# Conditioning loads moved to GpSimd's queue, the value weights split before the query rotation, and two partial sums of squares added on VectorE

## The chip, the cores and the metric

The kernel runs on one core of a Trainium2 chip. The metric is the device time of one execution in microseconds (us). It works from SBUF, with TensorE (PE) writing into eight PSUM banks; VectorE (DVE), ScalarE (ACT), GpSimd (POOL) and SyncE (SP) work beside it. DMAs are issued from the queues of SP, ACT and POOL, each in the order of the program: an instruction that waits holds everything behind it on its queue.

## What is computed

One encoder block over 1024 tokens of width 1024 in fp32. Two branches share an input projection; their gated sum is projected, and a SwiGLU layer follows. All norms are scaled and shifted by a conditioning vector `ada`.

```python
ada = silu(c) @ w_ada + b_ada                    # 6 x 1024 values
sh1, sc1, gt1, sh2, sc2, gt2 = split(ada, 6)
h = rms(x, g_pre_mix) * (1 + sc1) + sh1
q_lat, kv_lat, k_rope_raw, u, gates = split(h @ w_in)
a = mla(q_lat, kv_lat, k_rope_raw, ...)          # w_uq, w_uk, w_uv, rotation, softmax, w_o
b = s5(u, ...)                                   # state-space scan, gelu, w_glu
x = x + gt1 * rms((sig(gate_a) * a + sig(gate_b) * b) @ w_mix_out, g_post_mix)
h = rms(x, g_pre_ffn) * (1 + sc2) + sh2
x = x + gt2 * rms((silu(g) * up) @ w_ffn_out, g_post_ffn)
```

## The kernel before

Activations lie transposed, channels on partitions, in tiles of 128 channels by 1024 tokens; `halves` are the two times 512 tokens. Every product is made exact by splitting: `mm3` (lines 201 to 203) runs three matmuls, high by high, high by low, low by high. `WStream.split` (lines 183 and 184) casts a raw weight tile to its high half on ACT and subtracts it on VectorE for the low half. `get(ahead)` hands out the next tile and splits up to `ahead` tiles past it; there are two raw buffers and three split ones.

The order on each engine is that of the program, written by hand. Work of other kinds is threaded between the matmuls by generators: `s5_next` runs a step of the state-space branch, `norm_step` a step of the query norm and of the key/value norm.

The stages that the change touches:

- **Beginning** (lines 494 to 580). Eight tiles of x and eight of conditioning weights (`pw`) come in on SP's queue. ACT squares x; VectorE adds pairs; `norm_sums` (line 245) sums over channels with eight 128x1 matmuls for each added pair. `p_mm` (line 490) computes the conditioning of the upper four channel tiles on PE. For the lower four, `cond(k)` reduces two rows of w_ada against silu(c) on VectorE (`ada_reduce`, line 455). `norm_rstd` makes 1/rms, the matmuls of line 529 spread it, `h_prep` and `h_low` make the high and low halves of h. `tables` is a generator with small operations for the state-space branch.
- **Projection tiles 18 to 25** (the loop with `ADA0`, `QN0`). After the matmuls of a tile, `done` takes two sigmoids on ACT (line 954) and stores them; `flush()` issues the loads that `later` has put aside, on ACT's queue (line 147); `ada_do()` reduces the tiles that were asked for one projection tile before (`ada_reduce2`, line 462); then the next are asked for with `ada_load` or `ada_load2`, into buffers that the state-space branch no longer needs (er/ei, mr/mi, tz/r); then `norm_step`.
- **Query, key and value weights.** `uq_nope` makes four tiles of queries, `split_store` (line 1016) evicts each half as a high and a low part and stores both. `uq_rope` makes the rotated part: two tiles on PE, then products with cos and sin on VectorE out of PSUM. `uk_half` and `uv_tiles` (lines 1101 to 1103, eviction in line 1107) alternate on PE. The PSUM pool gives four banks to each of its two tags, taken in turn. `y_chain` puts gelu on ACT and a subtraction on POOL in between.
- **Gate** (`glu`, eight tiles of 48 matmuls): each reduces one conditioning tile and asks for the next with `ada_load`, on POOL's queue but for the first. Attention and the feed-forward layer follow; only the buffer count of one load in attention changes there.

The handover of a conditioning tile, as it stands before:

```python
        proj_tile(i, done)          # two sigmoids and their stores at the end
        flush()                     # issues what later() has put aside, on ACT
        if i >= QN0:
            ada_do()                # VectorE reduces those tiles
            ...                     # ada_load2: later(x, a["wada"][i][:, c])
            norm_step()
```

Of the kernel before, what the change touches and what calls it, by code (L numbers as in the profile page):

```python
# [13 lines left out]
ALU = mybir.AluOpType  # L14
# [6 lines left out]
KD = D // P  # L21
# [69 lines left out]
def _body(tc, a, out):  # L91
# [373 lines left out]
    with ExitStack() as p0:  # L465
        xp = pool("xp", stack=p0)
        x2 = pool("x2", bufs=1, stack=p0)
        tp = pool("s5t", stack=p0)
        sp = tp.tile([P, 96], F32, name="sp")
        SY.dma_start(sp, a["s5a"])  # L470
        xT = xp.tile([P, KD, S], F32, name="xT")
        rs = xp.tile([P, S], F32, name="rs")
        gsc = xp.tile([P, KD], F32, name="gsc")


        PK = KD // 2
        sq = [h_tile(F32, "sq") for _ in range(KD)]
        pw = [h_tile(F32, "pw") for _ in range(KD)]
        ptiles = [i for k in range(PK, KD) for i in (8 + k, k)]

        def p_load(*js):
            for j in js:
                SY.dma_start(pw[j], a["wadk"][ptiles[j]])

        def p_mm(*js):
            for j in js:
                i = ptiles[j]
                o = i - 8 - PK if i >= 8 else i
                for k in range(KD):
                    PE.matmul(pada[:, o:o + 1], pw[j][:, k * P:(k + 1) * P], silc[:, k:k + 1],  # L490
                              start=(j == 0 and k == 0), stop=(j == KD - 1 and k == KD - 1))

        for k in range(4):
            SY.dma_start(xT[:, k, :], a["xT"][k])
        p_load(0, 1)
        for k in range(4, KD):
            SY.dma_start(xT[:, k, :], a["xT"][k])
        p_load(2, 3)
        SY.dma_start(sil, a["c"].partition_broadcast(P))
        nxt = [[ada_tile(x2, 8), ada_tile(x2, 0)]]  # L500
        win.load(1)
        p_load(4, 5)
        win.load(1)
        p_load(6, 7)
        SY.dma_start(dd, a["s5d"])

        sums = ps_s5()
        prs = [ps_s5(), ps_s5()]
        pada = ps_s5()
        tables = s5_tables(tp, sp)  # L510
        next(tables)
        A_.activation(silc, vecs[:, 85:93], AF.Silu)
        for k in range(KD):
            A_.activation(sq[k], xT[:, k, :], AF.Square)
            if k % 2:
                tt(sq[k], sq[k - 1], sq[k], ALU.add)
                norm_sums(sums, sq[k], k == 1, k == KD - 1)
            if k == 3:
                next(tables)
                p_mm(0, 1)  # L520
        A_.activation(sil, sil, AF.Silu)
        dg = [x2.tile([P, HF], F32, name="dg", tag="dg", bufs=2) for _ in range(2)]
        rc = norm_rstd(sums, D, NJ)
        for h in range(2):
            norm_diag(rc[:, 4 * h:4 * h + 4], dg[h])
        next(tables)
        p_mm(2, 3)
        for h in range(2):
            PE.matmul(prs[h], ones, dg[h], start=True, stop=True)
            A_.copy(rs[:, halves[h]], prs[h])  # L530
        p_mm(4, 5, 6, 7)
        hhi, hlo = zip(*((h_tile(F32R, "hhi"), h_tile(F32R, "hlo")) for _ in range(KD)))

        def cond(k):
            ada_reduce(x2, nxt[0].pop(0), 8 + k)
            yield
            ada_reduce(x2, nxt.pop(0)[0], k)
            stt(gsc[:, k:k + 1], ada[:, 8 + k:9 + k], 1.0, g_pre[:, k:k + 1], ALU.add, ALU.mult)

        def h_prep(k, cs=(slice(0, S),)):  # L540
            for c in cs:
                stt(xT[:, k, c], xT[:, k, c], gsc[:, k:k + 1], rs[:, c], ALU.mult, ALU.mult)
                A_.activation(hhi[k][:, c], xT[:, k, c], AF.Identity, bias=ada[:, k:k + 1])

        def h_low(k, cs=(slice(0, S),)):
            for c in cs:
                stt(hlo[k][:, c], xT[:, k, c], ada[:, k:k + 1], hhi[k][:, c].bitcast(F32), ALU.add, ALU.subtract)

        for _ in cond(0):
            pass  # L550
        uw = [win.get(0, 0)]
        win.load(1)
        nxt.append([ada_tile(x2, 9), ada_tile(x2, 1)])
        h_prep(0, halves)
        uw.append(win.get(0, 0))
        h_low(0, halves)
        win.load(1)
        nxt.append([ada_tile(x2, 10), ada_tile(x2, 2)])
        win.keep[3] = lambda: [x2.tile([P, D], F32R, name=n) for n in ("w3hi", "w3lo")]
        uw.append(win.get(0, 0))  # L560
        for _ in cond(1):
            pass
        nxt.append([ada_tile(x2, 11), ada_tile(x2, 3)])
        uw.append(win.get(0, 0))
        tt(ada[:, 8 + PK:8 + KD], pada[:, 0:PK], b_ada[:, 8 + PK:8 + KD], ALU.add)
        tt(ada[:, PK:KD], pada[:, PK:KD], b_ada[:, PK:KD], ALU.add)
        stt(gsc[:, PK:KD], ada[:, 8 + PK:8 + KD], 1.0, g_pre[:, PK:KD], ALU.add, ALU.mult)
        h_prep(1)
        ups = [[f() for _ in range(2)] for f in (ps_mm, ps_mm, ps_s5, ps_s5)]
        for k in range(KD):  # L570
            if k:
                cd = cond(k + 1) if k + 1 < PK else iter(())
                next(cd, None)
                h_low(k)
                for _ in cd:
                    pass
                if k + 1 < KD:
                    h_prep(k + 1)
                for _ in range((0, 0, 0, 1, 2, 2, 2, 2)[k]):
                    next(tables, None)  # L580
            if k == 4 or k == 5:
                win.load(1)
            for m in (range(4) if k < KD - 1 else (3, 0, 1, 2)):
                for h, c in enumerate(halves):
                    mm3(ups[m][h], uw[m], hhi[k][:, c], hlo[k][:, c], k, k == 0, k == KD - 1)
        for _ in tables:
            pass
# [354 lines left out]
    def ada_load2(tags):  # L942

        i = ada_rest.pop(0)
        t = [s5b.tile([P, 512], F32, name=n, tag=n, bufs=tags[2]) for n in tags[:2]]
        for x, c in zip(t, halves):
            later(x, a["wada"][i][:, c])
        ada_live.append((t, i))

    for i in range(10, 26):  # L950
        def done(ps, i=i):
            for h in range(2):
                t = ev.tile([P, HF], F32, name="ev", tag="ev")
                A_.activation(t, ps[h], AF.Sigmoid)
                A_.dma_start(gdram[i - 10, :, h * HF:(h + 1) * HF], t)
        proj_tile(i, done)
        flush()
        if ADA0 <= i < QN0:
            ada_do()
            if i < QN0 - 1:  # L960
                ada_load(ADAN, nr, "nr", None, None)
        if i >= QN0:
            ada_do()
            for tags, first in ADA_TAGS:
                if first <= i < 25:
                    ada_load2(tags)
            if i == QN0:
                norms.append(q_norm())
            if i == KN0:
                norms.append(kv_stats())  # L970
            norm_step()
# [18 lines left out]
    yp = pool("y", side="right", stack=y_es)  # L990
    kvp = pool("kv", stack=r_es)
    rp = pool("rp", stack=r_es)
    sg = pool("sg", bufs=3, stack=r_es)
    csb = [rp.tile([P, S], F32, name=f"cs{i}") for i in range(2)]
    G.memset(vhi[:, :, :, 64:66].bitcast(F32), 1.0)
    G.memset(vlo[:, :, :, 64:66].bitcast(F32), 0.0)
# [69 lines left out]

    def uq_rope():

        w = win.get()
        pss = [dense_tile(w, i, 3, qhi, qlo) for i in range(2)]  # L1070
        qr = [qkd["qr"][e].rearrange("(h a r) s -> a h r s", a=2, r=16) for e in range(2)]
        yield
        prev = []
        for h, c in enumerate(halves):
            for i, op in enumerate((ALU.subtract, ALU.add)):
                ti = rp.tile([P, HF], F32, name="qra", tag="qra", bufs=3)
                u = rp.tile([P, HF], F32, name="qrb", tag="qrb")
                tt(ti, pss[i][h], csb[0][:, c], ALU.mult)
                tt(u, pss[1 - i][h], csb[1][:, c], ALU.mult)
                tt(ti, ti, u, op)  # L1080
                prev.append((ti, SCALE, [qr[e][i][:, :, c] for e in range(2)]))
                if len(prev) > 1:
                    split_store(*prev.pop(0))
            yield
        for p in prev:
            split_store(*p)
# [31 lines left out]
    def glu(m):  # L1118
# [2 lines left out]
        pa = dense_tile(w, 0, 4, yhi, ylo)  # L1121
        pg = dense_tile(w, 1, 4, yhi, ylo)
        ada_do()
        ada_load(min(GLU_ADA[m], len(ada_rest) - 8), gp, "wada", 3, G if m else None)
        flush()
        gb = gbs.pop(m)
        sgm = gp.tile([P, S], F32, name="sgm", tag="sgm")
# [191 lines left out]
    for i in range(len(steps) + LAG):  # L1319
# [14 lines left out]
            max_row(mh_)  # L1334
        if i in ATT_ADA:
            ada_do(1)
            ada_load(min(1, len(ada_rest) - 8), gp, "wada", 3)
        if i == NJ:
            gp_es.close()
            op = pool("o", side="right", stack=o_es)  # L1340
# [472 lines left out]
```

## Time and profile before

| | us |
|---|---|
| median of 3 runs | 1736.61 (1736.26 to 1737.35) |
| the profiled execution | 1737.2 |
| its span, first to last instruction | 1735.4 |

The profile is of one execution. Its page gives busy times by engine and by line; the trace behind it can be asked for waits (who waited for whom), timelines (instructions in order of time, with the idle time before each and what ended it), windows (busy time and granted TensorE clock of a stretch) and tiles. All times of the trace count from the span's start. In the rows, PE is TensorE's matmuls, an engine name with a q is its queue of DMA issues, `x32` counts merged instructions, and `L245` is line 245 of the kernel. Durations of neighbouring matmuls overlap; their pace is the distance between starts. The granted clock is 1.00 at 2.4 GHz and 0.50 at 1.2 GHz.

### The profile page before, as it was taken

To read this page: it belongs to the slowest core of one execution; us is meant where nothing else is said; L and a number is where in the kernel's file an instruction comes from. 1 tells how busy PE (TensorE), PEld (TensorE's weight loads), DVE (VectorE), ACT (ScalarE), POOL (GpSimd) and SP (SyncE) were. 2 spreads that over 40 slices of the span, in tenths; PEclk is the share of its full clock that TensorE was granted. 3 is DMA by queue.
4 is the path that set the end of the run, shared out by engine and by line. 5 is a ranking of instruction groups with operands and counts; after the bars stand their busy time and mean duration, and the time that the engine had idled before them with its cause. 6 is when DMAs were issued, how large, how long until landed. Compare 5 with 4: busy or idle time off the path is not lost.

```text
span 1735.4 us, 19440 instructions
## 1 busy us (share of the span) xinstructions
PE 1639.5 (94%) x7486; PEld 1325.3 (76%) x7486; DVE 976.7 (56%) x1613; ACT 553.1 (32%) x743; POOL 147.9 (9%) x191
## 2 busy tenths in 40 slices
PE   7989999986869999999999999999999999999995
PEld 7868887875648867776777777888888888888875
DVE  4978898844574777885455565222322322323367
ACT  3242312222252147767233344321111121111243
POOL 0340000000031000000233220000000000000002
PEclk9899999987889999999999999999999999999998
DMA  6342333452878541420443252212211111111234
GB/s 260 121 119 96 111 102 96 132 171 93 277 233 265 153 126 34 98 44 13 153 133 128 79 200 94 99 58 72 71 55 52 61 38 48 60 32 46 83 119 148
DMA packets 92540, 189.67 MB, mean 109 GB/s; under 512 B 19992, under 2 KB 36504, under 8 KB 92448
## 3 DMA queue, kind: packets, MB, share of 16 engines
q1 hardware_dynamic: 57920, 120.62, 22.8%
q10 hardware_dynamic: 31424, 58.34, 9.7%
q0 software_dynamic: 3104, 9.47, 1.8%
q8 instruction: 59, 0.97, 0.2%
q14 instruction: 33, 0.27, 0.1%
HBM read 148.61 MB, written 39.78 MB: 109 GB/s over the span
## 4 chain that ended last, share of the span: by engine, by line
PE 69%; DVE 17%; DMA 5%; ACT 5%; issue 3%; ACTq 1%; SPq 0%; DVEq 0%; POOLq 0%
PE mm L203 17%; PE mm L202 17%; PE mm L201 17%; DVE t L66 4%; PE sc L1251 2%; PE sc L1252 2%; PE sc L1253 2%; DVE wlo L66 2%; PE pv L1277 1%; PE pv L1276 1%; PE pv L1278 1%; ACT whi L183 1%; PE mm L1390 1%; PE mx L1199 1%; PE s L245 1%
## 5 line engine op out<-in xcount | busy, mean ns | idle before, releaser
L202 PE MATMUL mm<-mh,whi 128*128 128x512 f32 x736 | 288.9, 393 | 4.9 <-DVE mh L74 3.1
L203 PE MATMUL mm<-mh,wlo 128*128 128x512 f32 x736 | 288.9, 393 | 2.2 <-DVE wlo L66 2.1
L201 PE MATMUL mm<-mh,whi 128*128 128x512 f32 x736 | 289.6, 394 | 0.3 <-ACT whi L183 0.3
L66 DVE TENSOR_TENSOR wlo<-wraw,whi 128x1024 fp32r<-128x1024 f32 (+1 forms) x128 | 155.9, 1235 | 77.9 <-ACT whi L183 77.9
L66 DVE TENSOR_TENSOR silu<-mm,silu 128x512 f32<-128x512 f32 x44 | 30.4, 692 | 277.1 <-PE mm L203 270.9
L183 ACT CAST whi<-wraw 128x1024 fp32r<-128x1024 f32 (+1 forms) x128 | 129.9, 1035 | 165.0 <-PE mm L202 137.0
L202 PEld LDWEIGHTS mm<-mh,whi 128*128 128x128 f32 x736 | 139.0, 189 | 38.1 <-DVE mh L74 6.9
L203 PEld LDWEIGHTS mm<-mh,wlo 128*128 128x128 f32 x736 | 139.1, 189 | 33.1 <-DVE wlo L66 4.3
L201 PEld LDWEIGHTS mm<-mh,whi 128*128 128x128 f32 x736 | 139.3, 189 | 30.8 <-ACT whi L183 0.9
L201 PE MATMUL mm<-hhi,whi 128*128 128x512 f32 x384 | 159.1, 414 | 1.2 <-ACT ev L600 1.2
L202 PE MATMUL mm<-hlo,whi 128*128 128x512 f32 x384 | 154.5, 402 | 3.9 <-DVE hlo L74 3.9
L203 PE MATMUL mm<-hhi,wlo 128*128 128x512 f32 x384 | 154.8, 403 | 0.0
L201 PE MATMUL mm<-fhi,whi 128*128 128x512 f32 x304 | 118.8, 391 | 0.0
L202 PE MATMUL mm<-flo,whi 128*128 128x512 f32 x304 | 118.5, 390 | 0.0
L203 PE MATMUL mm<-fhi,wlo 128*128 128x512 f32 x304 | 118.3, 389 | 0.0
L66 DVE TENSOR_TENSOR mr<-mm,mr 128x512 f32<-128x512 f32 (+1 forms) x88 | 56.3, 641 | 97.1 <-PE mm L203 97.0
L66 DVE TENSOR_TENSOR plo<-p,phi 128x1024 fp32r<-128x1024 f32 x64 | 78.3, 1224 | 38.6 <-ACT phi L1257 38.3
L1609 ACT CAST fhi<-silu 128x512 fp32r<-128x512 f32 x44 | 27.3, 620 | 220.6 <-DVE silu L66 220.6
L202 PEld LDWEIGHTS mm<-hlo,whi 128*128 128x128 f32 x384 | 74.4, 194 | 21.8 <-DVE hlo L74 4.8
L201 PEld LDWEIGHTS mm<-hhi,whi 128*128 128x128 f32 x384 | 74.7, 194 | 19.9 <-issue 2.1
L203 PEld LDWEIGHTS mm<-hhi,wlo 128*128 128x128 f32 x384 | 74.1, 193 | 18.1
L1256 ACT ACTIVATE p<-sc 128x1024 f32<-128x1024 f32 x64 | 65.7, 1026 | 63.2 <-PE sc L1253 63.2
(517 smaller groups left out, 2951.2 us busy)
## 6 DMA issues: line engine op xcount, KB each, us to landing
wraw<-in_wfi SPq DMA_DIRECT2D x58, 512.0 KB
wraw<-in_win SPq DMA_DIRECT2D x26, 512.0 KB
wraw<-in_wfo SPq DMA_DIRECT2D x20, 512.0 KB
gdram<-ev ACTq DMA_DIRECT2D x32, 256.0 KB
wada<-in_wada POOLq DMA_DIRECT2D x15, 512.0 KB, 5.3
wraw<-in_wmix SPq DMA_DIRECT2D x10, 512.0 KB
xT<-in_xT SPq DMA_DIRECT2D x8, 512.0 KB
pw<-in_wadk SPq DMA_DIRECT2D x8, 512.0 KB
```

What stands on the lines that cost most here:

```text
L66: return self.eng.tensor_tensor(o, a, b, op=op)
L183: A_.copy(hi, t)
L201: PE.matmul(ps, whi[:, c], rhi, start=first, stop=False)
L202: PE.matmul(ps, whi[:, c], rlo, start=False, stop=False)
L203: PE.matmul(ps, wlo[:, c], rhi, start=False, stop=last)
L245: PE.matmul(ps[:, j:j + 1], src[:, j * P:(j + 1) * P], ones[:, 0:1], start=first and j == 0, stop=last and j == w - 1)
L1199: PE.matmul(pieces[j], qt["qhi"][b][0:96, t * P:(t + 1) * P], qt["khi"][b][0:96, halves[j]], start=True, stop=True)
L1251: PE.matmul(ps[:, c], kh[0:97, kc], qh[0:97, c], start=True, stop=False)
L1252: PE.matmul(ps[:, c], kh[0:96, kc], ql[0:96, c], start=False, stop=False)
L1253: PE.matmul(ps[:, c], kl[0:96, kc], qh[0:96, c], start=False, stop=True)
L1256: A_.activation(p, ps, AF.Exp)
L1609: A_.copy(fh[:, c], t)
```

## The change

1. Beginning: of the four added pairs of squares, the first two are added to the second, and that to the third, on VectorE (`sq[3] += sq[1]`, `sq[5] += sq[3]`), so that `norm_sums` runs for two tiles and not four. A step of `tables` is moved in front of `norm_rstd`. The conditioning tiles 9, 1 and 10 are asked for with the first loads, 2, 11 and 3 one at a time behind the weight tiles. `cond(0)` and the split of the first weight tile move in front of the spreading of 1/rms.
2. Projection tiles 18 to 25: `ada_load` and `ada_load2` issue on GpSimd's queue at once, in place of `later`.
3. `uq_rope` takes its weights with `get(2)`, which splits the tiles of w_uk and w_uv before the rotation. The store buffers of `split_store` go from three to five of each kind, the gate's conditioning buffers from three to one.

```diff
+        nxt += [[ada_tile(x2, 9), ada_tile(x2, 1)], [ada_tile(x2, 10)]]
         SY.dma_start(dd, a["s5d"])
...
             A_.activation(sq[k], xT[:, k, :], AF.Square)
             if k % 2:
                 tt(sq[k], sq[k - 1], sq[k], ALU.add)
-                norm_sums(sums, sq[k], k == 1, k == KD - 1)
+            if k == 3 or k == 5:
+                tt(sq[k], sq[k - 2], sq[k], ALU.add)
+            if k >= 5 and k % 2:
+                norm_sums(sums, sq[k], k == 5, k == KD - 1)
             if k == 3:
                 next(tables)
                 p_mm(0, 1)
         A_.activation(sil, sil, AF.Silu)
+        next(tables)
         dg = [x2.tile([P, HF], F32, name="dg", tag="dg", bufs=2) for _ in range(2)]
         rc = norm_rstd(sums, D, NJ)
         for h in range(2):
             norm_diag(rc[:, 4 * h:4 * h + 4], dg[h])
-        next(tables)
         p_mm(2, 3)
+        for _ in cond(0):
+            pass
+        uw = [win.get(0, 0)]
+        win.load(1)
+        nxt[1].append(ada_tile(x2, 2))
         for h in range(2):
             PE.matmul(prs[h], ones, dg[h], start=True, stop=True)
             A_.copy(rs[:, halves[h]], prs[h])
         p_mm(4, 5, 6, 7)
...
-        for _ in cond(0):
-            pass
-        uw = [win.get(0, 0)]
-        win.load(1)
-        nxt.append([ada_tile(x2, 9), ada_tile(x2, 1)])
         h_prep(0, halves)
         uw.append(win.get(0, 0))
         h_low(0, halves)
         win.load(1)
-        nxt.append([ada_tile(x2, 10), ada_tile(x2, 2)])
+        nxt.append([ada_tile(x2, 11)])
...
-        nxt.append([ada_tile(x2, 11), ada_tile(x2, 3)])
+        nxt[-1].append(ada_tile(x2, 3))
...
         for x, c in zip(t, halves):
-            later(x, a["wada"][i][:, c])
+            G.dma_start(x, a["wada"][i][:, c])
...
-                ada_load(ADAN, nr, "nr", None, None)
+                ada_load(ADAN, nr, "nr", None)
...
-    sg = pool("sg", bufs=3, stack=r_es)
+    sg = pool("sg", bufs=5, stack=r_es)
...
-        w = win.get()
+        w = win.get(2)
         pss = [dense_tile(w, i, 3, qhi, qlo) for i in range(2)]
...
-        ada_load(min(GLU_ADA[m], len(ada_rest) - 8), gp, "wada", 3, G if m else None)
+        ada_load(min(GLU_ADA[m], len(ada_rest) - 8), gp, "wada", 1, G if m else None)
...
-            ada_load(min(1, len(ada_rest) - 8), gp, "wada", 3)
+            ada_load(min(1, len(ada_rest) - 8), gp, "wada", 1)
```

## Rows read from the trace of the kernel before

**Rows 1.** The page, part 1: engine, busy us, share of the span, instructions

```profile
PE 1639.5 (94%) x7486; PEld 1325.3 (76%) x7486; DVE 976.7 (56%) x1613; ACT 553.1 (32%) x743; POOL 147.9 (9%) x191
```

**Rows 2.** Waits of PE, 355 to 530 us: engine, line, waited for: us, times, longest

```profile
PE s L1101 <- ACT whi L183: 12.8, 1, 12.8
PE s L245 <- DVE vi L66: 7.0, 1, 7.0
PE s L871 <- DVE t L66: 6.5, 1, 6.5
PE mm L871 <- DVE gb L66: 4.7, 1, 4.7
PE s L245 <- DVE t L66: 4.2, 1, 4.2
PE mm L203 <- DVE wlo L66: 3.8, 2, 3.3
PE s L1102 <- DVE wlo L66: 2.1, 1, 2.1
PE mm L201 <- issue: 0.5, 1, 0.5
```

**Rows 3.** Timeline of ACT and DVE near 390 us; waits of all engines, 355 to 530

```profile
386.52 0.44 ACTq L147 DMA_DIRECT2D er<-in_wada  x1
...
391.55 0.69 DVE L462 SCALAR_TENSOR_TENSOR er<-er,sil 128x512 f32<-128x512 f32 x1 [17.39 <-DMA er<-in_wada]
...
DVE er L462 <- DMA er<-in_wada: 39.7, 5, 17.4
```

**Rows 4.** Windows: stretch, its length, PE busy (instructions), granted clock, DMA share, GB/s

```profile
374.60:379.90 5.30, 5.30 (x14) 0.50 0.55 175
397.60:400.40 2.80, 2.79 (x5) 0.50 0.10 17
419.90:427.40 7.50, 7.42 (x21) 0.50 0.27 87
445.20:448.10 2.90, 2.88 (x7) 0.50 0.90 278
459.30:465.10 5.80, 5.73 (x10) 0.50 0.85 284
499.10:502.70 3.60, 3.56 (x8) 0.50 0.79 275
540.00:560.00 20.00, 20.00 (x88) 1.00 0.99 254
```

**Rows 5.** Timeline of the beginning, PE, DVE, ACT: start, us, engine, operation, idle before

```profile
10.27 6.98 PE L245 MATMUL s<-ones,sq 128*128 128x1 f32 x32 [10.27 <-DVE sq L66]
41.15 10.55 PE L490 MATMUL s<-silc,pw 128*128 128x1 f32 x64
...
30.94 0.17 DVE L71 TENSOR_SCALAR nq<-s 128x8 f32<-128x8 f32 x1 [10.40 <-PE s L245]
42.95 1.23 DVE L66 TENSOR_TENSOR wlo<-wraw,whi 128x1024 fp32r<-128x1024 f32 x1 [2.79 <-ACT whi L183]
...
14.40 1.06 ACT L514 ACTIVATE sq<-xT 128x1024 f32<-128x1024 f32 x1 [2.78 <-DMA xT<-in_xT]
```

**Rows 6.** Timeline of DVE and ACT around the query rotation, 480 to 501 us

```profile
482.11 0.68 DVE L66 TENSOR_TENSOR qra<-mm,cs 128x512 f32<-128x512 f32 x1
493.17 0.68 DVE L66 TENSOR_TENSOR qrb<-s,cs 128x512 f32<-128x512 f32 x1
500.14 0.68 DVE L74 SCALAR_TENSOR_TENSOR sglo<-mm,sghi 128x512 fp32r<-128x512 f32 x1
...
495.17 1.98 ACT L183 CAST whi<-wraw 128x1024 fp32r<-128x1024 f32 x2
```

**Rows 7.** Tile wada, 500 to 700 us, its landings; timeline of DVE in the gate

```profile
DMA to landing us min/median/max: 5.3/7.5/10.7
...
564.02 0.69 DVE L66 TENSOR_TENSOR sgm<-mm,sgm 128x512 f32<-128x512 f32 x1 [4.51 <-ACT sgm L1129]
```

More of the change, by code (lines that the diff above doesn't have):

```diff
@@ L504, in _body, with cond @@
         p_load(6, 7)
+        nxt += [[ada_tile(x2, 9), ada_tile(x2, 1)], [ada_tile(x2, 10)]]
         SY.dma_start(dd, a["s5d"])
+        def cond(k):
+            ada_reduce(x2, nxt[0].pop(0), 8 + k)
+            yield
+            ada_reduce(x2, nxt.pop(0)[0], k)
+            stt(gsc[:, k:k + 1], ada[:, 8 + k:9 + k], 1.0, g_pre[:, k:k + 1], ALU.add, ALU.mult)
         sums = ps_s5()
@@ L532, in _body @@
         hhi, hlo = zip(*((h_tile(F32R, "hhi"), h_tile(F32R, "hlo")) for _ in range(KD)))
[L534 to L538, printed above, removed]
         def h_prep(k, cs=(slice(0, S),)):
```

## The prediction, made before the changed kernel was run

> **What bounds the kernel now.** I read the page first: TensorE (PE) is busy 94% of the span [rows 1], so the time lies where PE waits or runs slowly. The view of PE's waits, asked stretch by stretch, then shows where that is. In 355 to 530 us PE waits 42 us, in eight groups [rows 2]; before it (110 to 355) the same view lists under 3 us, and after it 3.1 us up to 700. This stretch holds the last projection tiles, the query and key/value (kv) norms, and the weights w_uq, w_uk, w_uv. The windows at the places behind these waits show the second half of the loss: the granted clock is 0.50, the lower of the two levels (1.2 GHz), for 2.8 to 7.5 us after each long wait, while an undisturbed stretch passes 88 matmuls in 20 us, 0.227 each, at 1.00 [rows 4]. At the lower level a 512-column matmul starts every 0.427 us (seen in the timeline as the starts of neighbours), so 47% of such a stretch is lost.
>
> Why PE waits is seen on VectorE (DVE) and ScalarE (ACT), not on PE. A conditioning tile (ada) is loaded by ACT's queue in flush(), which stands behind the two sigmoids of the next projection tile, and ada_do() stands right behind that flush: so VectorE meets the reduction before its load has been in flight at all. ACT issues er at 386.52 and DVE starts its reduction at 391.55 after 17.39 us idle; in all it waits 39.7 us in five places for er alone [rows 3]. VectorE works in order, so the norm's sums, 1/rms, diagonals and the low halves of weights stand behind each wait, and PE waits for exactly these (t, vi, gb, wlo in [rows 2]). The largest single wait, 12.8 us, is for the high half of w_uv: its cast runs at 495.17, last in an ACT queue that first serves gelu and query rotation [rows 2, 6].
>
> **Part 1, the beginning.** PE starts with 128x1 matmuls, 32 instructions in 6.98 us (0.218 each), and is never idle from 10.27 until the projection starts [rows 5]. Two of four sums (8 matmuls, 16 instructions, 3.49 us each) go: 6.98 off PE. Two adds of 128x1024 come to VectorE, 1.23 us each by the nearest operation of that size [rows 5], beside ACT's squares. PE now starts with p_mm(0, 1), whose weights are queued between the fourth and fifth block of x; the blocks arrive 1.3 us apart and the fifth is used at 14.40 [rows 5], so the first of the two is there at about 11.8: 1.5 us later than PE starts now. p_mm(0, 1) ends at 18.8. VectorE reaches its second sum at 20.3 (the add ending at 12.9, the new add, the table chunk of 3.8 us, two adds), so PE idles 1.5 us. 6.98 - 1.5 - 1.5 leaves 3.5 us, carried through p_mm(2, 3) to the spread of 1/rms. The table chunk put ahead of norm_rstd (3.0 us) and its sines go into the 10.40 us in which VectorE waits for that sum anyway [rows 5]; without this cover they would cost their 3.0. cond(0) fits beside p_mm(2, 3). The split of the first weight tile, now done between the copies of rs and the first scaling (VectorE idles 2.79, then 1.23 of work [rows 5]), is moved ahead: the scaling starts right behind the second copy, 2.1 us earlier. The three early ada loads queue behind all of p_load, where the DMA engines are free after some 31 us; they cost nothing there, and take two loads out of the way of the fourth weight tile. From the first scaling to the last low half of h VectorE is the chain, so both gains reach the end of the stage: **5.5 us**. Bounds: p_mm(4..7) now takes 10.55 for 64 instructions [rows 5]; at the 0.218 of the earlier ones it takes 13.9 and eats 3.4. So 2 to 6.
>
> **Part 2, ada loads on GpSimd's queue.** In these tiles POOL has only memsets, so each load goes out as soon as its buffer is free, which is when the reduction of the tile before has read it: one projection tile (48 matmuls, 11 us) ahead of its use. What waits behind them on POOL: the memset of vhi, the cos/sin and kr loads, first needed some 20 us later. The nearest landings of the same tensor from POOL are 5.3, median 7.5, at most 10.7 us [rows 7]; I take 7.5 (same queue, same source, half the size here); even 10.7 is under 11. Followed tile by tile with the durations of the trace: VectorE reduces at 364, as soon as its own queue lets it; the sum of the second half is ready at 368.9 where PE arrives at 368.5; the diagonal of q at 380 against PE at 384; kv's sum at 396.5 against 396.6; the low half of the first w_uq tile at 412.4 against 415.8; kv's diagonal at 424 against 423.6. So PE keeps 0.6 us of wait, and the clock should stay up. What is lost there now: 4.2 + 6.5 + 7.0 + 3.3 + 4.7 = 25.7 us of waits [rows 2], and of half clock 47% of 5.3, 2.8, 7.5, 2.9 and of the first 3.8 of 5.8 us, 10.5, with 0.9 for the sums right before the first of these: 11.4 us [rows 4]. 25.7 + 11.4 - 0.6 = **36.5 us**. The two loads before tile 20 give nothing: VectorE is next held by PE's block kernel at 341. Bounds: at 10.7 us the second lot of four tiles lands at 420, the diagonal is 2 us late and the clock falls once: 33; nothing waits at all: 37.
>
> **Part 3, w_uv split ahead, and five store buffers.** get(2) puts one more cast (1.0 [rows 6]) and subtraction (1.2) ahead of the rotation; w_uv's load is issued behind the split of the third w_uq tile, a good ten us before, and hides. From the end of kv's spread (463.1) to the gate (521.2) PE loses 18.5 us now: 12.8 + 2.1 + 0.5 (3.8 less 3.3) and 0.5 of issue [rows 2] and 2.6 of half clock [rows 4]. The high half no longer waits, so PE runs w_uk and w_uv for five units of 1.36 us; then it needs PSUM tiles that the rotation holds. VectorE frees those of the second half with the multiply that starts 11.1 us after the first (493.17 against 482.11 [rows 6]); the first eviction of w_uk now comes 18 us behind the rotation's start, 1.2 less with one split fewer behind it [rows 6]. So a wait of 5.4 us stays, with some 4 us of half clock behind it (1.9): 7.3 remain, **11 us** gained. Bounds: 4 (PE stands until the first eviction) to 16 (no wait). The buffers (3 to 5 for stores, 3 to 1 for the gate's ada tile) cover waits of ACT and VectorE for stores, during which PE runs on from 463 to 480 out of spare PSUM: nothing counted, and nothing lost if that cover goes but the same waits as now.
>
> **The sum.** 5.5 + 36.5 + 11 = 53.0. The profiled execution took 1737.2 (span 1735.4 and 1.8 around it), 0.6 over the median of the runs: 1737.2 - 53.0 = 1684.2.
>
> **Rivals.** *A, the loads land late.* GpSimd builds them beside a working VectorE and behind one another in order; if two of the five waits return at 5 us each with their clock, 14 us are lost: 1698. For: landings up to 10.7 [rows 7]. Against: 8 us of slack in most tiles. The Trainium skill (SBUF — State Buffer, "SBUF: two separate sides") speaks against this change: while VectorE runs a two-port operation, GpSimd cannot write descriptors, and a load from its queue stands still. By that rule the reductions here, with two SBUF inputs, hold only GpSimd's reads, so the sum would stand, and only copies and scalar operations between them would bring A; the landings of 5.3 to 10.7 beside such work agree with a mild hold at most.
> *B, the rotation holds everything.* w_uk and w_uv are evicted behind it in order; then part 3 gives 0 to 4: 1693.
> *C, another queue is only another queue.* Loads are no earlier in effect, ACT only loses 26 issues of 0.45 us that hide nothing: part 2 is 0, 1737.2 - 16.5 = 1721. Against: the 17.39 us wait begins long before its issue [rows 3]. The Trainium skill (DMA: Bandwidth & Descriptors, "Issuing engines are not separate DMA queues") says that only the time of issue is saved, usually little; that rule is this rival.
> *D, slower: one buffer for the gate's ada tile.* Each of seven loads now starts after the reduction before it and is due 9.5 us later (a gate tile of 48 matmuls at 0.227 less 1.4). VectorE then idles 4.51 us for ACT [rows 7], so landings to 14 us are free. Every us beyond costs 7; it outweighs 53.0 from 21.6 us, twice the largest landing seen; at 22.5, 1744.
>
> **How the numbers follow.** Forecast 0.66 (1678 to 1698, from the bounds of 39 to 59 together); A 0.14; B 0.12; C 0.05; D 0.03. The range 1672 to 1706 takes in the forecast, A and B, and leaves C and D out. A measurement here can tell 0.2% (3.5 us) from no change: faster 0.96, same 0.01 (D just short of its point), slower 0.03.
>
> **What the profile will show.** Right: no VectorE wait for er over 2 us; PE's waits on t, vi, gb under 1 us and the clock at 1.00 from 365 to 440; the gate starting some 53 us earlier; a PE wait of about 5 us between w_uv tiles. Wrong: a PE wait above 3 us before the query rotation (part 2), PE idle until the first eviction of w_uk (part 3), the projection's first matmul after 50 us (part 1), or VectorE waiting for wada in the gate (D).

## The result, and the profile of the changed kernel

| | before | changed |
|---|---|---|
| median of the runs compared, us | 1736.98 | 1684.56 (1677.54 to 1687.83) |
| ratio, 95% interval | | 0.9691, 0.966 to 0.9723 |
| the profiled execution, us | 1737.2 | 1684.47 |
| its span, us | 1735.4 | 1682.7 |

The change is 52.4 us faster; the forecast was 1684.2 out of a sum of 53.0. Where the time went is read from the page first, then from PE's waits of the same stretch as [rows 2].

The first part of the page (engine, busy us, share of the span, instructions); [rows 1] answer to it:

```profile
PE 1618.4 (96%) x7454; PEld 1309.0 (78%) x7454; DVE 977.7 (58%) x1615; ACT 552.5 (33%) x743; POOL 164.0 (10%) x221
```

PE's waits from 355 to 530 us, and windows (stretch, length, busy us and instructions of PE, PEld, DVE, ACT, POOL, granted clock, DMA share, GB/s):

```profile
PE s L1105 <- DVE qra L66: 5.2, 1, 5.2
PE mm L201 <- DVE sglo L74: 0.2, 1, 0.2
PE s L245 <- DVE t L66: 0.2, 1, 0.2
```

```profile
360.00:380.00 20.00, 19.82 (x94) 15.91 (x94) 8.76 (x26) 5.14 (x9) 2.15 (x4) 0.91 0.68 226
380.00:400.00 20.00, 20.00 (x96) 16.45 (x95) 17.34 (x39) 9.05 (x15) 6.72 (x13) 1.00 0.59 192
400.00:431.00 31.00, 31.00 (x134) 24.73 (x133) 23.24 (x60) 10.39 (x17) 3.94 (x9) 1.00 0.98 305
440.00:446.00 6.00, 1.58 (x7) 0.96 (x6) 5.96 (x6) 1.42 (x3) 2.88 (x2) 0.86 0.87 313
446.00:450.00 4.00, 3.25 (x8) 2.58 (x9) 3.84 (x6) 3.97 (x6) 1.74 (x1) 0.50 0.52 194
450.00:455.00 5.00, 4.98 (x20) 3.69 (x19) 4.48 (x6) 1.55 (x5) 0.88 (x1) 0.89 0.67 221
470.00:490.00 20.00, 20.00 (x88) 16.08 (x87) 10.69 (x14) 6.06 (x8) 5.75 (x5) 1.00 0.80 229
```

Of the eight groups of [rows 2], 42 us, one of 5.2 us is left that counts: the wait of the w_uv tiles for the query rotation, which the forecast had kept at 5.4. The granted clock is 1.00 where [rows 4] show 0.50, with two exceptions. One is the fall around that wait (0.86, 0.50 and 0.89 from 440 to 455). The other is short: in the window with 0.91 the clock is 0.60 and 0.55 from 362 to 366, right behind the 128x1 matmuls of the query norm's sum. A second execution of the same kernel (after_again below) has 1.00 from 360 to 380.

Why the others are gone is seen on POOL and VectorE (timeline: start, us, engine, line, operation, idle before it and what ended it):

```profile
356.33 0.54 POOL L951 DMA_DIRECT2D er<-in_wada  x1 [9.37 <-DVE er L462]
361.76 0.68 DVE L462 SCALAR_TENSOR_TENSOR er<-er,sil 128x512 f32<-128x512 f32 x1
381.04 0.68 DVE L462 SCALAR_TENSOR_TENSOR er<-er,sil 128x512 f32<-128x512 f32 x1
```

A load leaves POOL as soon as VectorE has read the buffer, and VectorE starts the reductions of er without a bracket, that is, without idle time: its 39.7 us of waits for er in [rows 3] are zero.

The start of stages in the traces of all kernels is used below, so it is shown once how it is read: the tile view of `yhi`, the gate's input, gives the first and last start of the gate's matmuls, first before, then changed.

```profile
L201 PE MATMUL mm<-yhi,whi x64: 392/398/401, 521.2 to 612.8; 128*128 128x512 f32 x64
```

```profile
L201 PE MATMUL mm<-yhi,whi x64: 392/398/401, 464.8 to 556.4; 128*128 128x512 f32 x64
```

With the tiles of h, kv and the attention scores in the same view, the span falls into five stretches (us, one profiled execution each):

| kernel | to the first projection matmul | to the first w_uk matmul | to the gate | to the first scores | to the end |
|---|---|---|---|---|---|
| before | 51.6 | 429.4 | 40.2 | 98.8 | 1115.4 |
| changed | 47.8 | 386.8 | 30.2 | 98.8 | 1119.1 |
| p1_only | 50.7 | 429.6 | 41.0 | 98.8 | 1117.1 |
| p2_only | 53.9 | 388.8 | 40.6 | 98.8 | 1124.9 |
| get2_only | 51.1 | 432.8 | 31.3 | 98.8 | 1117.4 |
| bufs_back | 48.2 | 388.7 | 31.3 | 98.8 | 1125.1 |
| after_again (changed) | 50.6 | 385.1 | 29.9 | 98.8 | 1123.3 |
| act_at_once | 50.8 | 397.8 | 29.8 | 98.8 | 1116.6 |
| pool_at_flush | 47.3 | 386.5 | 30.1 | 98.9 | 1122.3 |
| rot_late | 47.3 | 391.1 | 28.6 | 111.2 | 1123.9 |
| ylo_dve | 51.2 | 390.4 | 28.0 | 98.8 | 1126.2 |
| row_on_sp | 50.3 | 389.1 | 30.3 | 98.8 | 1113.1 |
| more_pool_loads | 54.2 | 430.8 | 40.2 | 98.8 | 1115.5 |
| before_row_on_sp | 54.2 | 429.5 | 40.8 | 98.8 | 1112.4 |

Before against changed, stretch by stretch: 3.8 + 42.6 + 10.0 + 0.0 - 3.7 = 52.7 us, the difference of the spans. Stretches with the same code differ by some 3 us between executions, so a column is read with that much doubt. In the first column the reason is seen: the last 64 of the 128x1 matmuls before the projection take 10.5 to 10.8 us in six of the executions and 13.65 in the other eight, with the old beginning (51.1 and 51.6 against 53.9 to 54.2) as with the new (47.3 to 48.2 against 50.3 to 51.2). Why there are two durations stays open. The last column is not flat either: the changed kernel gives 3.7 us of its gain back behind the first scores, where the change edits only a buffer count. That is followed up below.

### The profile page after: what moved, and what is told of

Same layout as the page of the kernel before. It is cut to its first block, busy times and chain, and to the rows that moved or that the text cites. A ratio compares the mean times of both kernels' runs of the same rounds, so it can differ in the third digit from the quotient of the medians.

```text
span 1682.7 us, 19415 instructions
## 1 busy us (share of the span) xinstructions
PE 1618.4 (96%) x7454; PEld 1309.0 (78%) x7454; DVE 977.7 (58%) x1615; ACT 552.5 (33%) x743; POOL 164.0 (10%) x221
## 3 DMA queue, kind: packets, MB, share of 16 engines
q0 software_dynamic: 5632, 17.86, 3.5%
## 4 chain that ended last, share of the span: by engine, by line
PE 65%; DVE 20%; ACT 5%; DMA 4%; issue 4%; ACTq 1%; SPq 0%; DVEq 0%; POOLq 0%
PE mm L203 17%; PE mm L202 17%; PE mm L201 17%; DVE t L66 5%; DVE wlo L66 2%; PE sc L1255 1%; PE sc L1256 1%; PE sc L1257 1%; PE pv L1281 1%; PE pv L1280 1%; PE pv L1282 1%; ACT whi L183 1%; DMA mxd<-mneg 1%; PE mx L1203 1%; DVE s L695 1%
```

## The experiments

Each ratio is to the kernel before, timed beside it on the same chip.

### The parts alone

p1_only is item 1 of the change on the kernel before, p2_only its item 2, get2_only this line of item 3:

```diff
-        w = win.get()
+        w = win.get(2)
         pss = [dense_tile(w, i, 3, qhi, qlo) for i in range(2)]
```

> The kernel before with the changed beginning alone (part 1). The forecast's 5.5 us gives 1737.0 - 5.5 = 1731.5. The trace of the changed kernel has the steps behind this stage 6.6 us earlier, which gives 1730.4 if all of it comes from part 1. Rival: the waits behind the beginning swallow it and nothing is left, 1737.0. The view of DVE in the beginning should show the first scaling of h some 7 us earlier.

> The kernel before with part 2 alone, the conditioning loads of the projection tiles issued on GpSimd's queue. The forecast's 36.5 us gives 1700.5. Rival C (another queue is only another queue): 1737.0. Rival A (two of five waits come back): 1714.5. No wait of DVE for er over 2 us, PE at a granted clock of 1.00 from 365 to 440 but for short dips.

> The kernel before with the split of w_uk and w_uv ahead of the query rotation alone (the one edit of get(2), buffers as before). The forecast's 11 us gives 1726.0, with a wait of PE of 5.4 us left between the tiles of w_uv. Rival B (PE stands until the first eviction of w_uk): a gain of 0 to 4 us, 1733.0 to 1737.0.

| | median, us | ratio, 95% interval | gain out of 1742.89 | forecast |
|---|---|---|---|---|
| p1_only | 1738.21 | 0.997, 0.9956 to 0.9984 | 5.2 (2.8 to 7.7) | 5.5 |
| p2_only | 1707.32 | 0.9797, 0.9779 to 0.9816 | 35.4 (32.1 to 38.5) | 36.5 |
| get2_only | 1734.5 | 0.9955, 0.9936 to 0.9973 | 7.8 (4.7 to 11.2) | 11 |

All three forecasts lie within the intervals, the third at its edge; rivals B (0 to 4 us for part 3) and C (0 for part 2) fall, and A for part 2 (1714.5) too. The trace of get2_only shows its mechanism plainly; PE's waits from 355 to 530, where 12.8 for `whi` stood in [rows 2]:

```profile
PE s L1101 <- DVE qra L66: 5.4, 1, 5.4
PE mm L871 <- DVE gb L66: 4.6, 1, 4.6
```

w_uv no longer waits for its cast but for the rotation, 5.4 us as forecast, and the wait for gb, which belongs to part 2, stands untouched. p1_only's own trace does not show its gain at the gate: the gate starts at 521.3 (before: 521.2), and PE's waits from 355 to 530 add up to 46 us in place of 42. So in that execution the waits behind the beginning swallowed the lead, as the rival said. Its time was 1739.0; the kernel before took 1737.2 in the profiled execution and 1737.3 to 1747.4 beside p1_only, so one pair of traces cannot decide 5 us. That part 1 gains is shown by the times alone.

The three gains sum to 48.4 us. The changed kernel was timed again on the chip of the next experiments: 1689.42 against 1743.48, 0.9695 (0.967 to 0.972), 53.2 us. The sum is 4.8 us short of that, which the intervals allow to be chance; but what is missing from the three kernels is the buffers, so these were tried.

> The changed kernel once more, beside the next three on one chip. The first comparison gave 0.9691 of the kernel before (0.966 to 0.9723). Three parts alone gave 5.2, 35.3 and 7.8 us, 48.3 together, and the changed kernel with the old buffers 0.9717: if the buffers matter, this run lies 4.5 us under the one with the old buffers (0.9691 against 0.9717 of the kernel before); if not, both are equal and the sum of the parts misses 5 us that only the parts together give.

### The buffers

```diff
-    sg = pool("sg", bufs=5, stack=r_es)
+    sg = pool("sg", bufs=3, stack=r_es)
-        ada_load(min(GLU_ADA[m], len(ada_rest) - 8), gp, "wada", 1, G if m else None)
+        ada_load(min(GLU_ADA[m], len(ada_rest) - 8), gp, "wada", 3, G if m else None)
```

(and the same in attention)

> The changed kernel with the buffers as before (three store buffers of each kind, three gate tiles). The forecast counts the buffers at nothing: 1684.6, the time of the changed kernel. Rival: the store buffers hold the rotation and part 3 needs them: 2 to 5 us slower, 1686.6 to 1689.6. Rival D would show here as faster: the gate's single buffer costs some of the seven loads, 1 to 10 us.

1693.36 us, 0.9717 (0.9696 to 0.9739). Against the changed kernel's 0.9695 the times alone can't decide, since the intervals overlap. The traces can: the first matmul of w_uq starts at 408.4 without the added buffers and at 408.3 in the changed kernel, and the gate at 468.2 and 464.8, so 3.3 us are lost in between (in after_again that stretch takes 56.2 us, in the changed kernel 56.5, without the buffers 59.8). All engines' waits from 400 to 440 us, first with the old buffers, then in the changed kernel from 400 to 436:

```profile
DVE sglo L74 <- DMA qnd<-sglo: 9.8, 2, 8.6
ACT sghi L1020 <- DMA qnd<-sghi: 9.4, 3, 7.5
...
PE mm L201 <- issue: 2.1, 1, 2.1
```

```profile
ACT kvhi L887 <- DMA qnd<-sghi: 2.5, 1, 2.5
DVE sglo L74 <- DMA qnd<-sglo: 2.4, 1, 2.4
```

With three store buffers ACT and VectorE stand 7.5 and 8.6 us before they can evict the query tiles, and PE loses 2.1 us in front of the next ones; with five, 2.5 and 2.4 us of such waits are left and PE loses nothing. The buffers are worth about 3 us, the expectation's rival (2 to 5); the forecast's nothing was wrong.

### Queue or moment of issue

Part 2 changes two things: the queue, and that the load is issued where it is asked for and not put aside until the next flush. act_at_once keeps ACT's queue and the early place; pool_at_flush takes POOL's queue and the late place.

```diff
-            G.dma_start(x, a["wada"][i][:, c])
+            A_.dma_start(x, a["wada"][i][:, c])
```

```diff
-            G.dma_start(x, a["wada"][i][:, c])
+            later(x, a["wada"][i][:, c], G)
```

(and likewise for the two tiles in `nr`; in pool_at_flush also for the gate's first load)

> The changed kernel with the conditioning loads of the projection tiles back on ACT's queue, but issued at once where they are asked for, not put aside until the next flush. Theory of the forecast (the moment of issue counts, not the queue): er still lands before it is due, the wait of DVE for er stays under 2 us each, and the time is the changed kernel's, 1684.6, or a few us over it where ACT stands for the buffer that VectorE has yet to read. Rival (only GpSimd's own queue does it, because ACT's is blocked either way): er waits and half clock return, up to 1684.6 + 36 = 1720.

> The changed kernel with these loads put aside until the flush as before, but issued there on GpSimd's queue. GpSimd has nothing in between that waits for the sigmoids, so its instructions run ahead of that place in the program: the loads should go out at the same moment as in the changed kernel, and the time is the same 1684.6. Rival: the place in the program decides, the loads go out a tile later and some 36 us return, 1720.

act_at_once: 1693.0, 0.9721 (0.9697 to 0.9745). pool_at_flush: 1692.26, 0.9709 (0.9682 to 0.9736). In the trace of pool_at_flush the loads leave at the same moments as in the changed kernel (the row shown above stood at 356.33), though the program asks for them a projection tile later:

```profile
346.60 0.54 POOL L148 DMA_DIRECT2D er<-in_wada  x1 [24.87 <-DVE t L66]
357.05 0.54 POOL L148 DMA_DIRECT2D er<-in_wada  x1 [9.38 <-DVE er L463]
```

So the place in the program is nothing by itself: an engine with nothing else to do runs ahead to it. On ACT the early place does most of the work: VectorE's waits from 340 to 470 us list none for er. But ACT, which has work of its own, now stands where the load must wait for its buffer. ACT's waits from 355 to 440 and PE's from 355 to 530:

```profile
ACT whi L183 <- DMA ei<-in_wada: 4.6, 1, 4.6
ACT qhi L887 <- DMA ei<-in_wada: 4.3, 1, 4.3
```

```profile
PE s L245 <- DVE vi L66: 3.0, 1, 3.0
PE s L245 <- DVE t L66: 2.3, 1, 2.3
```

Casts stand behind the issue, VectorE behind the casts, PE behind VectorE, and the granted clock falls to 0.83 on the average of 365 to 385. The first w_uk matmul comes at 448.6 against 435.7 in after_again, 12.9 us later. In p1_only, which has the same beginning and the old loads, it comes at 480.3, 44.6 us later than in after_again. Of these the moment of issue brings 31.7 (some 2 of them are the buffers': that matmul comes at 436.9 in bufs_back and at 434.6 in the changed kernel), and an engine that can afford to stand brings 12.9. In time act_at_once lost only some 4.5 us (the intervals overlap), since its stretch behind the first scores is 6.7 us shorter (1116.6 against 1123.3).

### The wait that is left

Two attempts at the 5.2 us for the rotation. rot_late makes its eight products first and its sums and stores between the w_uk and w_uv tiles (with three store buffers, to make room):

```diff
-                tt(ti, ti, u, op)
-                prev.append((ti, SCALE, [qr[e][i][:, :, c] for e in range(2)]))
...
+                rot.append((ti, u, op, [qr[e][i][:, :, c] for e in range(2)]))
...
             next(uv)
+        rot_store()
```

ylo_dve takes a neighbour away. In the changed kernel VectorE's operations with two SBUF operands take four times as long while GpSimd subtracts (timeline of POOL, then of DVE):

```profile
437.84 5.18 POOL L1045 TENSOR_TENSOR ylo<-nr,yhi 128x1024 fp32r<-128x1024 f32 x2 [24.80 <-ACT yhi L1040]
```

```profile
437.44 0.68 DVE L66 TENSOR_TENSOR qrb<-mm,cs 128x512 f32<-128x512 f32 x1
438.16 2.64 DVE L66 TENSOR_TENSOR qra<-qra,qrb 128x512 f32<-128x512 f32 x1
440.72 2.85 DVE L74 SCALAR_TENSOR_TENSOR sglo<-qra,sghi 128x512 fp32r<-128x512 f32 x1
443.49 0.68 DVE L66 TENSOR_TENSOR qra<-s,cs 128x512 f32<-128x512 f32 x1
```

```diff
-            gt(ylo[k], t, yhi[k].bitcast(F32), ALU.subtract)
+            tt(ylo[k], t, yhi[k].bitcast(F32), ALU.subtract)
```

> The changed kernel with the query rotation taken apart: its eight products out of PSUM first (four buffers of each kind), its four sums and stores one at a time behind pairs of w_uk and w_uv tiles; three store buffers of each kind to make room. Theory: PE's 5.2 us wait for the rotation and some 2 us of half clock behind it go, 1684.6 - 7 = 1677.6. Rival: VectorE is the bound there and the wait only moves to the evictions behind, 1684.6; or the three store buffers cost what the order gains.

> The changed kernel with the four subtractions of y_chain on VectorE in place of GpSimd. In the trace of the changed kernel VectorE's operations with two SBUF operands take 2.6 to 2.9 us in place of 0.69 while GpSimd subtracts beside them, in the midst of the query rotation, 6.4 us in all, and PE then waits 5.2 us for the rotation. Theory: without that neighbour the rotation ends 5.2 us earlier (6.4 less one subtraction of 1.2 us put in front of its second half), PE's wait and its 1.9 us of half clock go, and the time is 0.9695 of the kernel before less 5 to 7 us, a ratio of 0.9655 to 0.9665. Rival: the evictions behind the rotation are what PE waits for next, and the ratio stays at 0.9695.

rot_late: 1699.82, 0.9742 (0.9704 to 0.978), no gain, and rather slower than the changed kernel (the intervals overlap). PE's wait for the rotation is gone and the stretch from w_uk to the gate is 28.6 in place of 30.2, but from the gate to the first scores it takes 111.2 in place of 98.8. PE's waits from 436 to 580:

```profile
PE mm L203 <- DVE wlo L66: 2.9, 3, 1.8
PE mm L201 <- issue: 2.5, 1, 2.5
PE mm L201 <- DVE sgm L66: 2.4, 1, 2.4
PE mm L201 <- DVE sglo L74: 2.2, 2, 1.9
```

In VectorE's timeline the last sum and store run at 475.97 and 477.44, and the low half of a gate weight, for which PE waits 1.8 us, only at 479.28, behind them; the granted clock is 0.83 from 456 to 466 and 0.75 from 476 to 486. What was put off was owed at the gate's start: the rival of its expectation (the wait only moves), and worse than it. The second and fourth of the rows above lie in front of the gate, and the three store buffers may have a part in them (bufs_back has such a row of 2.1). In the gate itself, 467 to 578, PE waits 5.6 us where the changed kernel waits none, and the clock falls a second time (0.57 from 521 to 529).

ylo_dve: 1692.83, 0.9718 (0.9694 to 0.9743), no gain. Its mechanism is there: the rotation's operations take 0.68 each, and PE waits 1.9 us for it. But GpSimd, free earlier, runs ahead to the products of `k_rope`, and these now fall on the kv norm (POOL, then DVE):

```profile
436.65 2.70 POOL L1045 TENSOR_TENSOR kr<-kr,kt 32x1024 f32<-32x1024 f32 x1
```

```profile
437.05 2.85 DVE L74 SCALAR_TENSOR_TENSOR nr<-nr,vecs,sgm 128x512 f32<-128x512 f32 x1
```

There 0.74 had been enough. PE now stands in front of the first w_uk matmul, where the changed kernel has no wait:

```profile
441.60 0.47 PE L201 MATMUL mm<-kvhi,whi 128*128 128x512 f32 x1 [3.56 <-issue]
```

The stretch behind that matmul is 2 us shorter. The theory's number was not met, and the rival's ratio of no gain was, by another path: the contention moved, it did not go.

### Where part of the gain went back

Of the 3.7 us that the last stretch lost in the changed kernel, 2.0 lie behind PE's last matmul. That matmul ends at 1726.3 of 1735.4 before and at 1671.6 of 1682.7 in the changed kernel, so 9.1 and 11.1 us ahead of the end. What grew there is a drain: GpSimd's queue is drained before the program ends. The view of the kernel's closing line gives its three drains (ns, min, median, max), before, then changed:

```profile
L1807 POOLq DRAIN  x3: 46/93/2976, 1731.2 to 1735.1; - x3
```

```profile
L1811 POOLq DRAIN  x3: 46/102/5421, 1676.4 to 1682.4; - x3
```

The long one takes 2.33 us with 18 DMAs issued by GpSimd in the program (before_row_on_sp), 2.97 to 2.98 with 26 (before, p1_only, get2_only, act_at_once), 4.77 with 48 (row_on_sp), 5.26 with 54 (more_pool_loads), 5.42 to 5.43 with 56 (the changed kernel and the others with part 2) and 5.51 with 57 (pool_at_flush): some 0.08 us for each. With 26 or fewer the last output stores end later than the drain, and nothing is lost; the 30 loads of part 2 cost 2.0 us there.

The other part lies in attention. Behind the first scores PE waits for one row of 4 KB, the negated maxima of a head, that goes out to memory and comes back into one partition of `qhi`. PE's wait for it from 530 to 900 us, and the row's times from DMA to landing (min, median, max), before and then after_again:

```profile
PE sc L1251 <- DMA qhi<-mxd: 2.1, 2, 1.7
```

```profile
DMA to landing us min/median/max: 1.7/1.9/3.3
```

```profile
PE sc L1255 <- DMA qhi<-mxd: 5.5, 2, 3.5
```

```profile
DMA to landing us min/median/max: 1.7/3.0/5.2
```

By the row's median, PE's longest wait and the last stretch the traces fall into two groups without overlap. In the five with the conditioning loads on ACT's queue (before, p1_only, get2_only, act_at_once, more_pool_loads) the row's median is 1.8 to 2.6 us, PE's longest wait for it 1.7 to 2.4, and the last stretch 1115.4 to 1117.4. In the seven with them on POOL's queue and the row there too (changed, after_again, p2_only, bufs_back, pool_at_flush, rot_late, ylo_dve) they are 2.8 to 3.3, 3.3 to 3.8, and 1119.1 to 1126.2. The groups are less clear by other numbers. PE's waits for the row from 530 to 900 us add up to 2.1 to 5.6 us in the first group and 4.0 to 6.7 in the second, and from the first scores to the last matmul, without the drain, it is 1104.6 to 1108.3 and 1108.0 to 1114.9. Three runs asked why.

```diff
-        G.dma_start(qt["qhi"][h % NQK][96:97].bitcast(F32), mxd[h:h + 1, :])
+        SY.dma_start(qt["qhi"][h % NQK][96:97].bitcast(F32), mxd[h:h + 1, :])
```

(row_on_sp on the changed kernel, before_row_on_sp on the kernel before), and on the kernel before, beside each load that ada_load2 issues in tiles 20 to 24:

```diff
+                    for _ in range(2):
+                        x = const.tile([P, 8], F32, name="xx", tag="xx", bufs=4)
+                        G.dma_start(x, a["wada"][i][:, 0:8])
```

> The changed kernel with the load of the row of maxima in attention (4 KB into one partition of qhi) on SyncE's queue in place of GpSimd's. In the traces with the conditioning loads on GpSimd's queue this row lands after 2.8 to 3.1 us (median) and PE's longest wait for it is 3.3 to 3.8 us; in three of the four with those loads on ACT's queue it is 1.9 to 2.2 us and a longest wait of 1.7 to 2.4 us; from the first scores to the end the former take 1119 to 1125 us, the latter 1115 to 1117. Theory: GpSimd's queue has become slower for this row, and another queue gives 3 to 7 us back, a ratio of 0.9655 to 0.968. Rival: the row is late for what it waits for on the writing side (11 to 12 us), SyncE's queue holds weight loads behind it, and nothing is gained or some us are lost, 0.9695 to 0.973.

> The kernel before with 28 further loads on GpSimd's queue in the projection tiles 20 to 24, each of 8 values per partition into a tile that nothing reads. Theory (the number of earlier loads on that queue makes the row of attention late): from the first scores to the end 1119 us or more in place of 1115.4, PE's longest wait for the row over 3 us, and the time 3 to 7 us over the kernel before, 1.002 to 1.004. Rival (the number of loads is not it): 1115 to 1117 us there and a ratio of 1.000.

> The kernel before with the row of maxima in attention loaded on SyncE's queue. In the changed kernel this edit gave a ratio of 0.9647 against 0.9695 without it, 0.48%, and took PE's wait for the row from 5.5 to 0.6 us. Theory (the change has made the row slower on GpSimd's queue, and so pays some of its gain back there): in the kernel before, where this stage and all behind it take 1115 to 1117 us against 1113 with the edit in the changed kernel, only 2 to 4 us are to be had, a ratio of 0.998 to 0.999. Rival (the row costs the same in both kernels): the same 0.48% here, 0.995.

row_on_sp: 1681.58 against 1741.25, 0.9647 (0.9621 to 0.9673), the fastest kernel of the study. PE's wait for the row, again from 530 to 900:

```profile
PE sc L1255 <- DMA qhi<-mxd: 0.6, 1, 0.6
```

before_row_on_sp: 1736.53 against 1741.94, 0.9963 (0.9948 to 0.9979), with the same row of 0.6. The edit is worth 0.48% in the changed kernel (from 0.9695) and 0.37% in the kernel before. That the row on SyncE's queue is better is shown in both. That the change made it worse is what the traces say (last stretches of 1112.4 and 1113.1 with the edit, 3 us under the kernel before and 6 to 10 under the changed one; of these 6 to 10 the shorter drain is 0.7). The times do not show it: the two gains can't be told apart, and of the numbers expected for before_row_on_sp the rival's 0.995 (the row costs the same in both kernels) lies within the interval, the theory's 0.998 just outside.

more_pool_loads: 1746.8, 1.0034 (1.002 to 1.0048). The time is where its theory put it, but the trace is not: the last stretch is 1115.5, the row's median 1.8 us. The mere number of loads on POOL's queue is not what makes the row late. It does lengthen the drain, and the end comes 10.9 us behind the last matmul in place of 9.1, so 1.8 us of this kernel's slowdown are explained. (These were small ones: the page counts 4000 packets on that queue, 3104 before and 5632 with part 2.) What makes the row land 1 us later when large loads went over the queue more than 140 us earlier stays open, and so does the rest of the slowdown of more_pool_loads, which is 5.9 us in all by the ratio.

## Why the prediction was right, point by point

**What bounds the kernel** was read rightly: nearly all of the gain up to the first scores lies in the waits of [rows 2], the clock behind them, and the beginning.

**Part 1**, 5.5 us forecast, 5.2 (2.8 to 7.7) measured alone. Its steps came within 0.2 us; the timeline of PE and of DVE in the changed kernel:

```profile
11.76 6.95 PE L490 MATMUL s<-silc,pw 128*128 128x1 f32 x32 [11.76 <-DMA pw<-in_wadk]
20.13 6.99 PE L245 MATMUL s<-ones,sq 128*128 128x1 f32 x32 [1.41 <-DVE sq L66]
37.36 10.54 PE L490 MATMUL s<-silc,pw 128*128 128x1 f32 x64
...
36.52 0.75 DVE L74 SCALAR_TENSOR_TENSOR xT<-xT,gsc,rs 128x512 f32<-128x512 f32 x1 [1.98 <-ACT rs L545]
```

Forecast were 11.8, 20.3, 1.5 us idle, and 10.55 for p_mm(4..7). VectorE's first scaling of h, expected some 7 us earlier in p1_only, starts at 36.37 in place of 44.10. The bound of 13.9 for p_mm(4..7) did not come in this execution, but 13.65 did in after_again, the same kernel, and in p1_only. The projection then starts at 50.6 and 50.7, which the prediction had named as a sign of being wrong ("after 50 us"). It is none, since the kernels with the old beginning show both durations too (p2_only: 13.65, and 53.9). Like compared with like, the projection starts some 3 to 4 us earlier, and the rest of the gain comes behind it.

**Part 2**, 36.5 forecast, 35.4 (32.1 to 38.5) alone. "The two loads before tile 20 give nothing" holds. VectorE waited 2.88 us for `nr` before and does not now, but PE gains nothing by it. Two of its rows, in front of these reductions and behind them, before, then changed:

```profile
333.05 1.95 PE L677 MATMUL s<-u,w 128*128 128x128 f32 x16
340.53 0.47 PE L734 MATMUL s<-mr,bp 64*32 64x128 f32 x16
```

```profile
325.20 1.95 PE L681 MATMUL s<-u,w 128*128 128x128 f32 x16
332.68 0.48 PE L738 MATMUL s<-mr,bp 64*32 64x128 f32 x16
```

PE is 7.85 us ahead at both, and VectorE, early now, waits 1.05 us for PE's second row. These 7.85 us are more than the 5.5 forecast for part 1; what else is in them was not followed. What the term left out is the drain: p2_only's gate starts 37.9 us earlier (483.3 against 521.2), and 2.0 of that are lost at the end. Rival A did not come: the page gives a median of 3.7 us from issue to landing for the ten loads of er from POOL, half of the 7.5 that was taken. The Trainium skill (SBUF — State Buffer, "SBUF: two separate sides") would have a load from GpSimd stand still beside VectorE's two-port operations. The landings of er, 2.9 to 5.7 us, show no such hold; but VectorE ran almost only operations with two inputs beside them, so for copies this case does not test it. Rival C fell, and act_at_once says how much the moment of issue brings. The Trainium skill (DMA: Bandwidth & Descriptors, "Issuing engines are not separate DMA queues") states that another engine only saves the time of issue, usually little. The trace agrees that it is the issue, 0.54 us on POOL, but on an engine in order the issue includes the wait in front of it, and that was most of the gain (31.7 of 44.6 us in the comparison above).

**Part 3**, 11 forecast, 7.8 (4.7 to 11.2) alone and 9 to 10 in the traces (40.2 to 41.0 from w_uk to the gate become 31.3). The wait of 5.4 that was to stay came as 5.2, with the half clock behind it. The value was some 1 to 3 us too high.

**The buffers** at nothing: the step that failed most clearly, about 3 us. The text had placed the waits for stores at 463 to 480, under PE's run out of spare PSUM. That cover, as it seems, existed in the kernel before because PE was late; with the waits of part 2 gone, the evictions of the query tiles became what was late next (the rows of bufs_back above).

**D**, the gate's single buffer, came as a wait but not as a loss: four waits of VectorE for wada, 10.0 us, longest 5.2 (all of DVE's from 465 to 640 us), while the gate's stretch is 98.8 in both kernels:

```profile
DVE wada L455 <- DMA wada<-in_wada: 10.0, 4, 5.2
```

The prediction had named any such wait as a sign against it. That was too strict: by its own reckoning landings up to 14 us were covered, and the longest was 11.1.

**The sum** was right within 1 us by errors of both signs, so its closeness is in part luck. In the pair of traces PE leads by 7.9 us in front of this stretch where 5.5 was forecast, and gains 48.5 from there to the gate where 47.5 was forecast; in the latter the buffers (about 3 us, counted at nothing) are set against a part 3 that was too high. The gate started 56.4 us earlier; 52.7 arrived. The prediction had not looked at the stages behind the gate, because the change hardly touches them: 3.7 us went back there, 2.0 of them in the drain.

## What to carry to other kernels

A load that stands behind an engine's own work is late by that work. Issue it from an engine that has nothing to wait for, and its place in the program hardly matters. When waits of that size go, cost again what they covered: small buffers and neighbours on a shared port that were free before are next in line, and stages behind the change can hand some of the gain back. A queue that looks free can have a price at the end of the program: compare the time behind the last matmul too.

## What the runs showed of the hardware

- VectorE's operations with both operands in SBUF stand still beside GpSimd's elementwise ones: 2.64 to 2.85 us in place of 0.68 to 0.74. The two GpSimd operations from 437.84 end at 440.25 and 443.02, and the slow ones on VectorE 0.55 us behind each, at 440.79 and 443.57. Moved away from one place, the same contention came up at the next. The Trainium skill (SBUF — State Buffer, "SBUF: two separate sides") calls the shared port a lock that one side holds for a whole instruction; the trace agrees.
- A 4 KB row into one partition costs PE up to 3.8 us on GpSimd's queue and 0.6 on SyncE's. The Trainium skill (DMA: Bandwidth & Descriptors, "SWDGE vs HWDGE vs iDMA") states that SyncE's descriptors are made by hardware with a faster setup than GpSimd's in software; the runs agree in sign, and show nothing of where in the path the time goes.
- The drain of GpSimd's queue at the program's end takes some 0.08 us for each DMA that GpSimd issued: 2.33, 2.98, 4.77, 5.26, 5.42 and 5.51 us with 18, 26, 48, 54, 56 and 57 of them.
